# The opening of a two-layer diffusion kernel: half of the first modulation quarter ahead, key weights by quarters, two conditioning units between keys and values, query weights split later

## The chip, the cores and the metric

One core of one Trainium2 chip. The metric is the device time of one execution in microseconds (us); times in the trace count from the start of the profiled span. Engines are named as in the profile: PE (TensorE), PEld (its weight loads), DVE (VectorE), ACT (ScalarE), POOL (GpSimd), SP (SyncE, which issues the loads here).

## What is computed

Two layers over 512 latent tokens and 256 context tokens of width 1024. The change lies in the first layer's attention, cut here to what matters:

```python
mx = split(silu(c) @ ada_w[0] + ada_b[0], 6)        # shift, scale, gate, shift, scale, gate
mc = split(silu(c_ctx) @ ada_w[0] + ada_b[0], 6)
h_x = rms_norm(x, norm1_g[0]) * (1 + mx[1]) + mx[0]
h_c = rms_norm(ctx, norm1_g[0]) * (1 + mc[1]) + mc[0]
q, k, v = split(h_x @ w_qkv, [1024, 1280])          # 16 query heads, 4 key and value heads of 64
k_c, v_c = split(h_c @ w_qkv[:, 1024:], 2)          # context keys and values
q, k = rope(rms_norm(q, q_gain)), rope(rms_norm(k, k_gain))
out = softmax(window and context scores, sink) @ values @ w_o
```

After it come a SwiGLU feed-forward part, and a second layer with retention. The output is the latent stream.

## The kernel before, in words

Streams are held transposed, as 8 tiles of 128 channels by tokens (`res`). Products are done in three passes: a weight tile is split into a rounded part `whi` and a rest `wlo` (a cast on ACT, a subtraction on DVE), the moving operand likewise, and whi x hi, wlo x hi, whi x lo are summed in PSUM (`mm3`).

The opening goes through these steps. Eight latent tiles are loaded; ACT squares them, DVE adds the squares (`add_square`, L210, L211), and PE multiplies the sum with a matrix of ones (`rms`, L218); ACT and DVE make the normalising factor from it (`neg_half_rstd`, L101, L196 to L198). The modulation of the first norm (shift and scale) comes in four quarters of 256 channels: `ada_quarter` multiplies a quarter's four loaded tiles (`adan`) with the conditioning columns `ccol` (32 small matmuls, L338), ACT copies the result out (L341), PE turns it by two transposes (L345), and DVE adds the bias and makes the columns for one stream (L351, L352, L114). A function `fill` is issued between the product and the transposes. `hidden0` then makes two hidden tiles: DVE multiplies (L437), ACT adds the shift and rounds (L438), DVE makes the rest (L442). `keys(s, q)` (L451) adds what quarter q gives to the keys of stream s (0 latent, 1 context; 12 matmuls of 512 or 256 columns), `values(s, q, tiles)` (L465) the same for the values, 6 matmuls of 256 columns for each tile of 128 tokens. `high` and `low` (L380, L383) split the key and value weights; `busy` (L422) issues matmuls whose result nobody reads, to fill PE's waits. The order of all this on PE, DVE and ACT is the order in which the code is written (`tc.manual_schedule`).

Behind it a second block fixes PE alone: the last values, four conditioning units (`ada_unit`, L308 product, L311 copy, L315 transpose, L318 columns on DVE), the factors of the three key tiles (`key_factor`, L562) and the key operands (`key_parts`, L571 to L575). From there a scheduler orders the engines by dependencies and place in the program. `make_q` gives for a pair of heads the query tile as four pieces: `first`, `second` and `third` are the products for latent and context (L148 to L150) and `shape` (L628 and L629 on ACT read the product, L633 to L636 apply the rotary positions, L642 to L645 split the result), `norms` is six tiny matmuls (L654) that sum the squares, and DVE steps that end the use of their PSUM bank (L657). Pieces are placed among the steps of the attention blocks (`steps`); the query weights are loaded and split (L140 on ACT, L141 on DVE) when `make_q` is called. PSUM tiles named `pj` are two banks in turn: a third use waits for the readers of the first. The raw weight tiles `wraw` are two buffers in turn, and SP issues all loads in program order.

## Time and profile before

| what | value |
| --- | --- |
| median of 3 runs | 1747.66 us (1744.28 to 1747.7) |
| the profiled execution: its own time, its span | 1748.38 us, 1746.6 us |
| mean granted PE clock of the span | 0.997 |
| PE, DVE, ACT busy | 1717.8, 1335.8, 845.3 us |
| loads of the first 44 us: DMA share, first 19.71 us and then to 43.96 us | 0.90, 0.98 |

A row of the timeline gives the start in us, the busy time in us, engine, line, operation, the tiles out<-in with their shape, the number of instructions, and in brackets how long the engine had been idle and which engine, tile and line (or which load) released it. A PE matmul shows its whole latency as busy, so the start of the next one tells how fast they follow. A row of the stages gives the stretch, its length, the busy time and count of PE, PEld, DVE, ACT and POOL, the granted PE clock, the mean DMA share and GB/s.

### The profile page before, as it was taken

To read this page: it belongs to the slowest core of one execution; us is meant where nothing else is said; L and a number is where in the kernel's file an instruction comes from. 1 tells how busy PE (TensorE), PEld (TensorE's weight loads), DVE (VectorE), ACT (ScalarE), POOL (GpSimd) and SP (SyncE) were. 2 spreads that over 40 slices of the span, in tenths; PEclk is the share of its full clock that TensorE was granted. 3 is DMA by queue.
4 is the path that set the end of the run, shared out by engine and by line. 5 is a ranking of instruction groups with operands and counts; after the bars stand their busy time and mean duration, and the time that the engine had idled before them with its cause. 6 is when DMAs were issued, how large, how long until landed. Compare 5 with 4: busy or idle time off the path is not lost.

```text
span 1746.6 us, 28180 instructions
## 1 busy us (share of the span) xinstructions
PE 1717.8 (98%) x11092; PEld 1537.3 (88%) x11092; DVE 1335.8 (76%) x2382; ACT 845.3 (48%) x1509; POOL 121.2 (7%) x266
## 2 busy tenths in 40 slices
PE   7999999999999999999998999999999999999999
PEld 5888887889999999999998888898898999999997
DVE  5797786478778787877899758758768898777774
ACT  5577686365434333342565534624525555445442
POOL 0023344000000000000010000000000100000000
PEclk9999999999999999999999999999999999999999
DMA  9510024142243434343433434433433224233322
GB/s 365 206 61 16 23 61 146 49 141 101 97 133 122 144 121 157 109 145 110 140 115 122 157 97 134 157 109 123 157 103 115 97 87 124 80 116 102 105 77 85
DMA packets 61476, 205.67 MB, mean 118 GB/s; under 512 B 6816, under 2 KB 7456, under 8 KB 61216
## 3 DMA queue, kind: packets, MB, share of 16 engines
q1 hardware_dynamic: 54432, 178.71, 31.1%
q0 software_dynamic: 6912, 25.17, 4.7%
q8 instruction: 87, 1.43, 0.3%
q14 instruction: 45, 0.37, 0.1%
HBM read 201.75 MB, written 2.10 MB: 117 GB/s over the span
## 4 chain that ended last, share of the span: by engine, by line
PE 42%; DVE 6%; DMA 2%; ACT 1%; issue 0%; ACTq 0%; DVEq 0%; SPq 0%
PE Y L935 6%; PE Z L1338 6%; PE Z L935 3%; PE Y L1325 3%; PE pj L149 2%; PE pj L148 2%; PE pj L150 2%; PE pj L1338 2%; DMA wraw<-in_wst_dram 2%; PE X L935 2%; PE X L1325 1%; DVE wlo L1257 1%; PE X L1338 1%; PE X L150 1%; PE X L148 1%; PE X L149 1%
## 5 line engine op out<-in xcount | busy, mean ns | idle before, releaser
L165 ACT CAST whi<-wraw 128x1024 fp32r<-128x1024 f32 x117 | 122.4, 1052 | 208.4 <-PE Z L150 71.0
L935 PE MATMUL Y<-aq,whi 128*128 128x384 f32 x640 | 174.0, 336 | 2.1 <-ACT hn L1080 2.1
L166 DVE TENSOR_TENSOR wlo<-wraw,whi 128x1024 fp32r<-128x1024 f32 x117 | 142.5, 1222 | 16.1 <-ACT whi L165 15.7
L254 DVE SCALAR_TENSOR_TENSOR res<-pj,mod,res 128x512 f32<-128x512 f32 (+1 forms) x102 | 74.3, 729 | 78.5 <-PE pj L150 77.5
L935 PEld LDWEIGHTS Y<-aq,whi 128*128 128x128 f32 x640 | 116.7, 188 | 4.1 <-ACT hn L1080 3.9
L141 DVE TENSOR_TENSOR wlo<-wraw,whi 128x1024 fp32r<-128x1024 f32 x76 | 92.7, 1221 | 27.8 <-ACT whi L140 26.8
L140 ACT CAST whi<-wraw 128x1024 fp32r<-128x1024 f32 x76 | 79.7, 1048 | 70.0 <-PE Z L150 24.8
L935 PE MATMUL Y<-aq,wlo 128*128 128x384 f32 x320 | 107.0, 334 | 0.0
L272 DVE CUSTOM_DVE_ANT_0 y<-adaw,crow,small_sb 128x1024 bf16<-128x1024 f32 x64 | 81.9, 1279 | 31.3 <-DMA adaw<-in_adaT_dram 31.1
L1256 ACT CAST whi<-wraw 128x1024 fp32r<-128x1024 f32 x56 | 58.7, 1050 | 74.1 <-PE Y L150 52.6
L1257 DVE TENSOR_TENSOR wlo<-wraw,whi 128x1024 fp32r<-128x1024 f32 x56 | 68.0, 1220 | 18.0 <-ACT whi L1256 17.8
L1338 PE MATMUL Z<-whi,sA 128*128 128x512 f32 x256 | 80.4, 390 | 0.0
L101 ACT ACTIVATE pr<-pr,stat,qs 128x513 f32<-128x513 f32 (+2 forms) x96 | 74.1, 775 | 10.9 <-DVE stat L732 9.6
L739 POOL TENSOR_SCALAR pr<-pr,stat 128x512 f32<-128x512 f32 (+2 forms) x96 | 66.5, 705 | 73.1 <-DVE stat L736 48.9
L148 PE MATMUL pj<-ax,whi 128*128 128x512 f32 x176 | 68.8, 391 | 0.5 <-DVE res L254 0.5
L150 PE MATMUL pj<-ax,whi 128*128 128x512 f32 x176 | 68.7, 390 | 0.0
L149 PE MATMUL pj<-ax,wlo 128*128 128x512 f32 x176 | 68.5, 389 | 0.0
L269 POOL DMA_DIRECT2D adaw<-in_adaT_dram x48 | 25.6, 533 | 515.4 <-DVE mod L272 421.8
L935 PE MATMUL Y<-sA,whi 128*128 128x256 f32 x304 | 60.6, 282 | 0.0
L935 PEld LDWEIGHTS Y<-aq,wlo 128*128 128x128 f32 x320 | 60.1, 188 | 0.1
L148 PE MATMUL pj<-act,whi 128*128 128x512 f32 (+1 forms) x156 | 60.0, 384 | 0.0
L149 PE MATMUL pj<-act,wlo 128*128 128x512 f32 (+1 forms) x156 | 59.9, 384 | 0.0
(583 smaller groups left out, 5428.0 us busy)
## 6 DMA issues: line engine op xcount, KB each, us to landing
wraw<-in_wst_dram SPq DMA_DIRECT2D x232, 512.0 KB, 3.7
adaw<-in_adaT_dram POOLq DMA_DIRECT2D x48, 512.0 KB, 3.9
wx<-in_wst_dram SPq DMA_DIRECT2D x28, 512.0 KB, 4.4
adan<-in_adaQ_dram SPq DMA_DIRECT2D x16, 512.0 KB, 7.7
adan<-in_adaN_dram SPq DMA_DIRECT2D x16, 512.0 KB, 7.1
res<-in_xT_dram SPq DMA_DIRECT2D x16, 256.0 KB, 4.9
q<-in_adaN_dram SPq DMA_DIRECT2D x16, 256.0 KB, 3.6
aq<-in_adaN_dram SPq DMA_DIRECT2D x12, 256.0 KB, 5.7
```

Of the source, the lines that this page charges most:

```text
L140: after(nc.scalar.copy(hi, raw), behind)
L141: after(nc.vector.tensor_tensor(lo, raw, hi, op=sub), low)
L148: after(nc.tensor.matmul(o, whi, xhi, start=first, stop=False), behind)
L149: nc.tensor.matmul(o, wlo, xhi, start=False, stop=False)
L150: return nc.tensor.matmul(o, whi, xlo, start=False, stop=last)
L165: nc.scalar.copy(hi, t)
L166: return nc.vector.tensor_tensor(lo, t, hi, op=sub)
L254: return nc.vector.scalar_tensor_tensor(res[d], o, mods[l, s][:, part, d:d + 1], res[d], mult, add)
L272: after(nc.vector.tensor_tensor_reduce(junk, w, cr[:, s * 1024:(s + 1) * 1024], 1.0, sm_t[:, C_ADAB + l * 48 + j:C_ADAB + l * 48 + j + 1], ...
L935: ins = nc.tensor.matmul(o, p, r, start=first and k + i == 0, stop=k == 3 and i == 2, skip_group_check=not first)
L1257: last_split[0] = nc.vector.tensor_tensor(lo, raw, hi, op=sub)
L1338: ins = nc.tensor.matmul(o, p, r, start=first and k + i == 0, stop=k == 3 and i == 2, skip_group_check=not first)
```

## The change

The opening is written in another order, and some pieces are cut smaller:

- The first quarter is done in halves by `first_quarter`. Its scale half is loaded first, multiplied, copied out by DVE and turned, and only then its shift half is multiplied, copied out by ACT and turned.
- The last of the eight squares is no longer added by DVE: PE multiplies it with the ones by itself, and adds the product of the sum of the other eight in the same bank. One `busy(SX)` goes.
- Key weights 0 and 1 are loaded and split by 256, 256 and 512 columns (before 256 and 768), and their loads change places with the context tiles'.
- `values`, `hidden0`, `rms(1)` and the context keys are placed otherwise; conditioning units 0 and 1 move from behind the last latent values to between the last keys; context values of quarters 0 and 1 move the other way.
- The raw weights of query tile 0 are loaded into two key tiles and not into a `wraw` buffer. The weights of query tiles 2 and up are split when a fifth piece, `weights`, is called: at once for tile 2, at step 2 of the group for the second tile of a group, and three steps ahead of the group for its first.

In the opening, PE's list was this up to the first key products (`y_241` is the sum of squares, `sq` in L345 the copy of the quarter):

```order
L422 MATMUL kvv<-res,ones_sb 128x512 x4
L218 MATMUL pT<-y_241,ones_sb 128x512
L338 MATMUL pT<-adan,ccol 32x128 x32
L422 MATMUL kvv<-res,ones_sb 128x256
L345 MATMUL pT<-const_sb,sq 128x128 x2
L422 MATMUL kvv<-res,ones_sb 128x512 x2
L451 MATMUL pj<-h,whi 128x512 x2
```

In the changed kernel PE's list at the same place is this (`sc` are the copies of the two halves, L335 the products, L480 the keys):

```order
L449 MATMUL kvv<-res,ones_sb 128x512 x4
L521 MATMUL pT<-sq,ones_sb 128x512
L522 MATMUL pT<-y_245,ones_sb 128x512
L335 MATMUL pT<-adan,ccol 32x128 x16
L353 MATMUL pT<-const_sb,sc 128x128
L335 MATMUL pT<-adan,ccol 32x128 x16
L449 MATMUL kvv<-res,ones_sb 128x256
L353 MATMUL pT<-const_sb,sc 128x128
L449 MATMUL kvv<-res,ones_sb 128x512
L480 MATMUL pj<-h,whi 128x512 x2
```

The transpose of the scales now stands between the two halves of the product. DVE's list at this place was before, from the last additions to the first hidden tiles (`hs`):

```order
L211 TENSOR_TENSOR y_241<-y_241,sq 128x512 x7
L197 SCALAR_TENSOR_TENSOR sq<-pT,sq 128x512
L198 SCALAR_TENSOR_TENSOR y_241<-sq,y_241 128x512
L351 TENSOR_TENSOR mod_74<-pT,small_sb 128x2x2
L352 TENSOR_TENSOR mod_74<-pT,mod_74 128x2x2
L114 SCALAR_TENSOR_TENSOR acol_78<-mod_74,gm_85 128x2
L437 SCALAR_TENSOR_TENSOR hs<-res,acol_78,y_241 128x512 x2
```

DVE's list there in the changed kernel:

```order
L211 TENSOR_TENSOR y_245<-y_245,sq 128x512 x6
L197 SCALAR_TENSOR_TENSOR sq<-pT,sq 128x512
L198 SCALAR_TENSOR_TENSOR y_245<-sq,y_245 128x512
L357 COPY sc<-pT 128x128
L343 TENSOR_TENSOR mod_74<-pT,small_sb 128x2
L344 TENSOR_TENSOR mod_74<-pT,mod_74 128x2
L114 SCALAR_TENSOR_TENSOR acol_78<-mod_74,gm_85 128x2
L464 SCALAR_TENSOR_TENSOR hs<-res,acol_78,y_245 128x512
L343 TENSOR_TENSOR mod_74<-pT,small_sb 128x2
L344 TENSOR_TENSOR mod_74<-pT,mod_74 128x2
L464 SCALAR_TENSOR_TENSOR hs<-res,acol_78,y_245 128x512
```

The copy of the scales stands behind both steps of the norm's factor, and the shift's two steps stand between the first and the second hidden tile. The second place is the second query tile (heads 2 and 3), behind the first one's sums of squares (`qs`). DVE had before, up to the end of those sums' use (L657):

```order
L197 SCALAR_TENSOR_TENSOR qs<-pj,qs 128x12
L575 TENSOR_TENSOR k<-res,k 64x512
L644 TENSOR_TENSOR q<-hn,q 64x512
L645 TENSOR_TENSOR q<-hn,q 64x512
L644 TENSOR_TENSOR q<-hn,q 64x256
L645 TENSOR_TENSOR q<-hn,q 64x256
L198 SCALAR_TENSOR_TENSOR qs<-qs 128x12
L574 TENSOR_TENSOR k<-res,k 64x512
L657 SCALAR_TENSOR_TENSOR qs<-pj,qs 128x12
```

DVE has now, up to the same step (L699) and on to the second tile's rotary step (L678) and a score (L773):

```order
L197 SCALAR_TENSOR_TENSOR qs<-pj,qs 128x12
L619 TENSOR_TENSOR k<-res,k 64x512
L198 SCALAR_TENSOR_TENSOR qs<-qs 128x12
L141 TENSOR_TENSOR wlo<-wraw,whi 128x1024
L699 SCALAR_TENSOR_TENSOR qs<-pj,qs 128x12
L675 STREAM_SHUFFLE y_1238<-hn 128x512
L703 TENSOR_SCALAR qs<-qs,nsink 128x6 x2
L676 TENSOR_TENSOR hn<-hn,rope_192 128x512
L677 TENSOR_TENSOR y_1238<-y_1238,rope_192 128x512
L773 ISA pr,stat<-S_1353,mask,qs 128x512
L773 ISA stat 128x1
L678 TENSOR_TENSOR hn<-hn,y_1238 128x512
```

A whole weight split (L141) stands ahead of L699 now, and a score ahead of the rotary sum L678. ACT had before, for the second query tile's product (`hn`, `sq`) and what followed:

```order
L628 ACTIVATE hn<-pj,qk_gain 128x512
L629 ACTIVATE sq<-pj 128x512
L628 ACTIVATE hn<-pj,qk_gain 128x256
L629 ACTIVATE sq<-pj 128x256
L101 ACTIVATE qs<-pj,small_sb 128x12
L101 ACTIVATE qs<-qs 128x12
L196 ACTIVATE qs<-qs 128x12
L642 CAST q<-hn 64x512
```

ACT has now:

```order
L670 ACTIVATE hn<-pj,qk_gain 128x512
L671 ACTIVATE sq<-pj 128x512
L670 ACTIVATE hn<-pj,qk_gain 128x256
L684 CAST q<-hn 64x512
L685 CAST q<-hn 64x512
L671 ACTIVATE sq<-pj 128x256
L684 CAST q<-hn 64x256
L685 CAST q<-hn 64x256
L101 ACTIVATE qs<-pj,small_sb 128x12
```

The context square L671 stands behind two casts that read L678's result. The diff, cut to its core:

```diff
     def ada_quarter_load(q):
-        w = []
-        for i in range(4):
-            w.append(T(st_p, 1024, "adan", 8))
+        w = [T(st_p, 1024, "adan", 8) for _ in range(4)]
+        for i in (2, 3, 0, 1) if q == 0 else range(4):
             nc.sync.dma_start(w[i], adaQ[q, i // 2, i % 2])
         return w
 
+    def quarter_product(o, w, part, ks):
+
+        for k2 in ks:
+            for j in range(4):
+                k = 2 * k2 + j // 2
+                c0 = (k % 4) * 256 + j % 2 * P
+                nc.tensor.matmul(o[32 * j:32 * j + 32, part * P:(part + 1) * P], ccol[:, k, :],
+                                 w[2 * part + k // 4][:, c0:c0 + P], start=k2 == 0, stop=k2 == 3)
+
+    def quarter_columns(q, t, s, parts=(0, 1)):
+        tv = t.rearrange("p (f h d c) -> p c h f d", f=2, h=2, d=2)
+        bias = sm_t[:, C_ADAB:C_ADAB + 16].rearrange("p (f d) -> p f d", f=2)[:, :, 2 * q:2 * q + 2]
+        f = slice(parts[0], parts[-1] + 1)
+        col = mods[0, s][:, f, 2 * q:2 * q + 2]
+        nc.vector.tensor_tensor(col, tv[:, s, 0, f], bias[:, f], op=add)
+        nc.vector.tensor_tensor(col, tv[:, s, 1, f], col, op=add)
+        if 1 in parts:
+            fold_gain(0, s, 0, 2 * q, 2 * q + 2)
+
+    def first_quarter(w, fill):
+
+        o, t = pT()[:, 0:256], pT()[:, 0:256]
+
+        def turn(part, rows):
+            nc.tensor.transpose(t[:, part * P:(part + 1) * P], rows, ident)
+
+        quarter_product(o, w, 1, range(4))
+        scales, shifts = (T(st_p, SC, "sc", 2)[:, :P] for _ in range(2))
+        nc.vector.tensor_copy(scales, o[:, P:])
+        turn(1, scales)
+        quarter_columns(0, t, 0, (1,))
+        quarter_product(o, w, 0, range(4))
+        nc.scalar.copy(shifts, o[:, 0:P])
+        fill()
+        turn(0, shifts)
+        return lambda: quarter_columns(0, t, 0, (0,)), lambda: quarter_columns(0, t, 1)
+
     def ada_quarter(q, w, fill):
 
         o = pT()[:, 0:256]
         for part in range(2):
-            for k2 in range(4):
-                for j in range(4):
-                    k = 2 * k2 + j // 2
-                    c0 = (k % 4) * 256 + j % 2 * P
-                    nc.tensor.matmul(o[32 * j:32 * j + 32, part * P:(part + 1) * P], ccol[:, k, :],
-                                     w[2 * part + k // 4][:, c0:c0 + P], start=k2 == 0, stop=k2 == 3)
+            quarter_product(o, w, part, range(4))
         rows = t_sq(256)
         nc.scalar.copy(rows, o)
         fill()
         t = pT()[:, 0:256]
         for part in range(2):
             nc.tensor.transpose(t[:, part * P:(part + 1) * P], rows[:, part * P:(part + 1) * P], ident)
...
     res0[1] = load_stream(1, 0, 4)
     wq.append(ada_quarter_load(1))
+    load_cols(0, quarters[1])
+    load_cols(1, quarters[1])
     res0[1] += load_stream(1, 4)
-    load_cols(0, REST)
-    load_cols(1, REST)
     load_cols(2, BACK)
+    load_cols(0, BACK)
+    load_cols(1, BACK)
     wq.append(ada_quarter_load(2))
...
-    q_raw = [w_raw()]
+    q_raw = [key_room()]
+    for i, c in enumerate((HEAD, BACK)):
+        nc.sync.dma_start(q_raw[0][i], wst[wpos[0]][:, c])
+    wpos[0] += 1
     wu = [unit_load(u) for u in UNITS[:2]]
...
             nc.vector.scalar_tensor_tensor(ts[-1], res0[s][k], acol[0, s, 0][:, k:k + 1], y, mult, mult)
+            for b in early if k == ks[0] else ():
+                b()
             nc.scalar.activation(h[s][k][0], ts[-1], AF.Identity, bias=mods[0, s][:, 0, k:k + 1])
...
     with tc.manual_schedule(engines={mybir.EngineType.PE, mybir.EngineType.DVE, mybir.EngineType.Activation}):
-        squares0(0, *range(KT))
+        squares0(0, *range(KT - 1))
+        last_square = t_sq(SX)
+        nc.scalar.activation(last_square, res0[0][KT - 1], AF.Square)
         for k in range(4):
             busy(SX, k)
-        rms(0, bank=pT)
+        tot = pT()
+        nc.tensor.matmul(tot, ones, last_square, start=True, stop=False)
+        nc.tensor.matmul(tot, ones, ssq[0], start=False, stop=True)
+        neg_half_rstd(ssq[0], t_sq(SX), tot, D)
 
         def first_fill():
             high(0, quarters[0])
             high(1, quarters[0])
             busy(SC)
 
-        c1 = ada_quarter(0, wq[0], first_fill)
+        c0, c1 = first_quarter(wq[0], first_fill)
         busy(SX)
-        busy(SX)
-        hidden0(0, 0, 1, between=(lambda: low(0, quarters[0]), lambda: low(1, quarters[0])))
+        hidden0(0, 0, 1, between=(lambda: low(0, quarters[0]), lambda: low(1, quarters[0])), early=(c0,))
         high(2, HEAD)
         c1()
         keys(0, 0)
         low(2, HEAD)
         squares0(1, 0, 1, 2, 3)
-        c1 = ada_quarter(1, wq[1], lambda: values(0, 0, (0,)))
-        high(0, REST)
-        values(0, 0, (1, 2, 3))
-        hidden0(0, 2, 3, between=(lambda: low(0, quarters[1]), lambda: high(1, REST), lambda: low(1, quarters[1])))
+        values(0, 0, (0,))
+        c1 = ada_quarter(1, wq[1], lambda: values(0, 0, (1,)))
+        high(0, quarters[1])
+        high(1, quarters[1])
+        values(0, 0, (2, 3))
+        hidden0(0, 2, 3, between=(lambda: low(0, quarters[1]), lambda: low(1, quarters[1])))
         c1()
         high(2, BACK)
         low(2, BACK)
         squares0(1, 4, 5, 6, 7)
+        high(0, BACK)
+        high(1, BACK)
+        low(0, quarters[2])
+        low(1, quarters[2])
         keys(0, 1)
         values(0, 1, (0, 1))
+        c1 = ada_quarter(2, wq[2], lambda: values(0, 1, (2,)))
+        hidden0(0, 4, 5)
         rms(1, bank=pT)
-        c1 = ada_quarter(2, wq[2], lambda: values(0, 1, (2,)))
         values(0, 1, (3,))
-        hidden0(0, 4, 5, between=(lambda: low(0, quarters[2]), lambda: low(1, quarters[2])))
-        c1()
         high(3, HEAD)
         low(3, HEAD)
+        c1()
+        keys(0, 2)
         hidden0(1, 0, 1)
-        keys(0, 2)
-        keys(1, 0)
-        values(0, 2, (0, 1, 2))
-        hidden0(1, 2, 3)
         low(0, quarters[3])
         low(1, quarters[3])
-        c1 = ada_quarter(3, wq[3], lambda: values(0, 2, (3,)))
+        c1 = ada_quarter(3, wq[3], lambda: values(0, 2, (0,)))
         c1()
         hidden0(0, 6, 7)
+        values(0, 2, (1, 2, 3))
+        keys(1, 0)
+        hidden0(1, 2, 3)
         high(3, BACK)
+        end = ada_unit(UNITS[0], wu[0])
+        keys(0, 3)
+        end()
+        hidden0(1, 4, 5)
+        keys(1, 1)
+        end = ada_unit(UNITS[1], wu[1])
+        hidden0(1, 6, 7)
         low(3, BACK)
-        keys(1, 1)
-        values(1, 0)
-        values(1, 1)
-        hidden0(1, 4, 5)
-        hidden0(1, 6, 7)
-        keys(0, 3)
         keys(1, 2)
+        end()
         last_key = keys(1, 3)
...
         after(values(0, 3), [last_key])
-        ends = [ada_unit(UNITS[0], wu[0])]
+        ends = [ada_unit(UNITS[2], wu[2])]
         rope_key(kn[0])
-        values(1, 2)
-        ends.pop()()
-        ends.append(ada_unit(UNITS[1], wu[1]))
         key_factor(0)
+        values(1, 0)
         ends.pop()()
         for e in range(2):
             kx[e] = key_parts(e, kn[0])
+        values(1, 1)
+        ends.append(ada_unit(UNITS[3], wu[3]))
+        key_factor(1, pO)
+        values(1, 2)
+        ends.pop()()
+        off_grid(akv, 16)
+        for e in range(2):
+            k1, k2 = key_parts(e, kn[1], "kc", 4)
+            kc[e], kc[2 + e] = ((k1[:, c], k2[:, c]) for c in HALVES)
+        off_grid(akv, 48)
         values(1, 3)
+        rope_key(kn[2])
+        key_last = key_factor(2)
         vt = []
         for t in range(6):
             v = T(akv, 256, "v", 6)
             nc.scalar.copy(v, kvv[t // 2][:, t % 2 * 256:t % 2 * 256 + 256])
             vt.append(v)
-        ends.append(ada_unit(UNITS[2], wu[2]))
-        key_factor(1)
-        off_grid(akv, 16)
-        for e in range(2):
-            k1, k2 = key_parts(e, kn[1], "kc", 4)
-            kc[e], kc[2 + e] = ((k1[:, c], k2[:, c]) for c in HALVES)
-        off_grid(akv, 48)
-        ends.pop()()
-        ends.append(ada_unit(UNITS[3], wu[3]))
-        rope_key(kn[2])
-        key_last = key_factor(2, pO)
-        ends.pop()()
...
+        def weights():
+            w.extend(cut(next_w(ap, 1, raw, behind, behind)))
+
         def first():
+            if not w:
+                weights()
             part(0, 0, 5)
...
-            steps[12 * g + r] = list(fs)
+            steps.setdefault(12 * g + r, []).extend(fs)
+        if g == 0:
+            a[4]()
+        else:
+            steps.setdefault(12 * g - 3, []).append(a[4])
+        steps.setdefault(12 * g + 2, []).append(b[4])
```

32 lines of the change are left out of this document (14 added, 18 removed).

## The prediction

> **What bounds the kernel now.** I read the page first (busy shares and slices), then a table of the stages of the opening, then the timelines of PE, DVE and ACT where PE waits. On the page:
>
> ```profile
> PE 1717.8 (98%) x11092; PEld 1537.3 (88%) x11092; DVE 1335.8 (76%) x2382; ACT 845.3 (48%) x1509; POOL 121.2 (7%) x266
> PE   7999999999999999999998999999999999999999
> ```
>
> PE is busy for 98% of the span, and only the first slice of 43.7 us falls below nine tenths. The profiled execution took 1748.38 us, of which the span is 1746.6. The lists of all engines agree from inside the attention stage on, before 330 us, so the change can act only ahead of that. The table of stages:
>
> ```profile
> 0.00:19.71 19.71, 12.53 (x82) 5.53 (x82) 9.03 (x21) 12.59 (x20) 0.64 (x9) 1.00 0.90 327
> 19.71:43.96 24.25, 21.63 (x218) 16.37 (x218) 16.93 (x45) 11.46 (x24) 0.00 (x0) 1.00 0.98 391
> 43.96:64.06 20.10, 19.62 (x198) 18.47 (x199) 14.63 (x41) 10.91 (x24) 0.00 (x0) 1.00 0.64 226
> 64.06:87.81 23.75, 23.46 (x340) 18.12 (x339) 18.05 (x47) 15.14 (x30) 0.00 (x0) 1.00 0.49 187
> 87.81:101.37 13.56, 12.25 (x82) 11.01 (x81) 13.20 (x27) 9.58 (x19) 0.30 (x2) 1.00 0.17 49
> 101.37:330.00 228.63, 227.04 (x1681) 182.98 (x1681) 171.12 (x557) 155.81 (x372) 83.29 (x190) 0.99 0.17 56
> ```
>
> The stages are the first norm and quarter; three quarters of latent keys and values; the rest of the keys; units and key operands with query tile 0; query tile 1; attention. Behind 43.96 PE idles little, except for 1.3 us in 87.81:101.37, where DVE is busy 13.20 of 13.56 us: there DVE sets the pace. What the change can win lies ahead of 44 us; whether it is kept is decided at 87 to 101 us.
>
> PE's rate isn't the busy time of one matmul, as two neighbours show:
>
> ```profile
> 84.07 0.39 PE L150 MATMUL pj<-h,k 128*128 128x512 f32 x1
> 84.30 0.39 PE L148 MATMUL pj<-h,k 128*128 128x512 f32 x1
> ```
>
> They start 0.23 us apart (0.235 over a long row of them), so 12 key products of 512 columns are 2.82 us; a value tile, 6 products of half the columns, I take at 0.71.
>
> **Step 1, the opening chain: +0.85 us.** PE, then DVE, then ACT:
>
> ```profile
> 12.45 1.13 PE L218 MATMUL pT<-y,ones_sb 128*128 128x512 f32 x2 [1.69 <-DVE y L211]
> 13.51 1.84 PE L338 MATMUL pT<-adan,ccol 128*32 128x128 f32 x48
> 15.95 0.64 PE L338 MATMUL pT<-adan,ccol 128*32 128x128 f32 x16 [0.60 <-DMA adan<-in_adaQ_dram]
> 17.09 0.44 PE L345 MATMUL pT<-const_sb,sq 128*128 128x128 f32 x2
> 19.71 0.50 PE L451 MATMUL pj<-h,whi 128*128 128x512 f32 x1 [0.47 <-ACT h L438]
> ```
>
> ```profile
> 16.38 0.69 DVE L198 SCALAR_TENSOR_TENSOR y<-sq,y 128x512 f32<-128x512 f32 x1
> 17.56 0.16 DVE L351 TENSOR_TENSOR mod<-pT,small_sb 128x4 f32<-128x4 f32 x1 [0.49 <-PE pT L345]
> 18.15 1.41 DVE L437 SCALAR_TENSOR_TENSOR hs<-res,acol,y 128x512 f32<-128x512 f32 x2
> ```
>
> ```profile
> 10.84 0.63 ACT L210 ACTIVATE sq<-res 128x512 f32<-128x512 f32 x1 [0.17 <-DVE y L211]
> 18.94 1.38 ACT L438 ACTIVATE h<-hs,mod 128x512 fp32r<-128x512 f32 x2 [1.29 <-DVE hs L437]
> 66.08 0.27 ACT L311 COPY sq<-pT 128x128 f32<-128x128 f32 x1 [1.27 <-PE pT L308]
> ```
>
> The last square is done at 11.47. Before, a last addition on DVE and one product with the ones follow, up to about 13.6. After, two such products (about 1 us each) follow from 11.5, also to about 13.6: the saved addition buys the added product, gain 0. The norm's two DVE steps end at 17.07 as before. The copy of the scales stands behind them on DVE. No row shows a 128x128 copy on DVE: it lies between 0.16 (the 128x4 step) and 0.69 (512 columns); I take 0.29, next to ACT's 0.27 for the same shape. It ends at 17.4, and here PE's order costs: the scale transpose (0.27) comes after that, and only then the shift half of the product, which before was over at 16.6. The 64 products took 1.84 + 0.64 less overlap, 1.9 in all; half is 0.94. So the shift product ends at 18.66, ACT copies to 18.99, PE turns to about 19.35 behind `busy`, DVE adds twice to 19.75 and makes the second `hs` by 20.47; ACT's first hidden tile ends about 20.5 and the first key product starts at 20.56 instead of 19.71. Bounds: +0.4 if the copy is 0.16 and PE's queue flows, +1.2 at 0.69. The ACT casts of key weights there are hidden under the wait for the shift; without it they would be 0.7.
>
> **Step 2, 19.71 to 43.96: -2.25 us.** Rows of PE:
>
> ```profile
> 23.09 1.96 PE L338 MATMUL pT<-adan,ccol 128*32 128x128 f32 x64
> 25.79 0.38 PE L345 MATMUL pT<-const_sb,sq 128*128 128x128 f32 x2
> 28.36 0.50 PE L451 MATMUL pj<-h,whi 128*128 128x512 f32 x1
> 34.63 0.67 PE L218 MATMUL pT<-y,ones_sb 128*128 128x256 f32 x2 [0.45 <-DVE y L211]
> 40.50 0.49 PE L451 MATMUL pj<-h,whi 128*128 128x512 f32 x1 [1.48 <-ACT h L438]
> 44.42 0.79 PE L451 MATMUL pO<-hc,whi 128*128 128x256 f32 x2 [0.46 <-ACT hc L438]
> ```
>
> The stage's work is three key quarters (8.46), eight value tiles (5.68), two quarter products (3.8), two pairs of transposes (0.5) and the context norm (0.6): 19.0 us of 24.25, so 5.2 are waits (more than the idle rows say, since an isolated matmul shows as 0.5 busy). Between transposes and first key product of a quarter lie 28.36 - 26.17 = 2.2 us (copying, columns, two hidden tiles on DVE and ACT). After, two value tiles (1.42) stand in quarter 1's gap, and the norm and one tile (1.3) in quarter 2's, leaving 0.75 and 0.85. About 0.45 each stays in the three key quarters, where a second hidden tile follows a first; more was there while the 768-column casts stood between. Left: 0.45 + 0.75 + 0.46 + 0.85 + 0.46, about 3.0; 5.25 - 3.0 = 2.25. Gone are the 1.48 at 40.50 and the norm's 0.45. Bounds: 1.2, if what DVE does between (the 1.2 us splits in the same queue) stretches the two gaps by 0.5 each, and 3.2, if only half a microsecond stays in each gap.
>
> **Step 3, 43.96 to 87.81: -1.85 us.** The work is the same in another order, 41.8 us by the rates. Of 43.85 us 2.0 are waits and tails; the 0.46 at 44.42 goes, since values stand ahead of the context keys, and the load's wait in the next row goes with the other tails, as units stand between keys:
>
> ```profile
> 73.94 0.65 PE L308 MATMUL pT<-adan,ccol 128*32 128x128 f32 x16 [0.29 <-DMA adan<-in_adaN_dram]
> 89.69 0.61 PE L654 MATMUL pj<-const_sb,sq 128*128 128x2 f32 x4 [0.84 <-ACT sq L629]
> 90.16 0.48 PE L148 MATMUL pj<-h,whi 128*128 128x512 f32 x1
> ```
>
> This asks unit 0's weights some 24 us earlier. Ahead of them and in them are about 16 MB; at 327 and then 391 GB/s the stages' rows give 15.9 MB by 43.96, so they land about 47, needed at 49; unit 1 (another 2 MB, 5 us) about 52.5, needed at 55. The margins are 2 to 3 us, and this is what the swapped key and context loads live on too: if they miss, PE waits by as much. I take 0 for that, bound +1. By steps 1 to 3 the first query tile's sums of squares end near 86.7, against 90.16 before: 3.45 ahead: 3.25 by the three steps, and 0.2 off the 0.84 that PE waits for the last square, which ACT reaches with one cast less ahead of it.
>
> **Step 4, query tile 1, 87 to 101: +2.25 us given back.** DVE:
>
> ```profile
> 88.18 0.73 DVE L633 STREAM_SHUFFLE y<-hn 128x512 f32<-128x512 f32 x1
> 88.80 1.21 DVE L141 TENSOR_TENSOR wlo<-wraw,whi 128x1024 fp32r<-128x1024 f32 x1
> 92.66 0.67 DVE L575 TENSOR_TENSOR k<-res,k 64x512 fp32r<-64x512 f32 x1
> 96.62 0.17 DVE L657 SCALAR_TENSOR_TENSOR qs<-pj,qs 128x12 f32<-128x12 f32 x1
> ```
>
> PE and ACT at its end:
>
> ```profile
> 96.94 0.36 PE L148 MATMUL pj<-hc,whi 128*128 128x256 f32 x1 [0.47 <-DVE qs L657]
> 101.37 0.47 PE L148 MATMUL pj<-h,whi 128*128 128x512 f32 x1
> ```
>
> ```profile
> 100.33 0.38 ACT L629 ACTIVATE sq<-pj 128x256 f32<-128x256 f32 x1
> ```
>
> From the first tile's shuffle to the end of L657 DVE needs 8.61 us; PE's context half waits for that end (0.47), as the bank is in use. Now one more weight split (1.21) and one key part (0.70) fall between: 10.5. The shuffle comes at about 83.5 (the key operands' work ends 4.7 earlier), so L699 ends at 94.15; PE stands there from 86.7 + 5.64 (24 products of 512 columns) + 0.95 (its other work) = 93.3: it waits 0.85. The context half ends near 97.0. Then ACT: the context square stands behind two casts that want L678, ahead of which DVE has shuffle 0.73, two small steps 0.36, two products 1.36, a score about 0.8 and the sum 0.69: 98.1. Two casts at the 0.63 of ACT's 512 columns and the square's 0.38 give 99.8, the last sums 0.45: 100.15 for the start of the third tile, against 101.37. Of 3.45 us 1.2 are left. Bounds: 0 given back, if PE reads other work in these waits, and 3.4, if L699 is a whole split later.
>
> **Step 5, the rest: 0.** Query tiles from the third on split their weights later; PE's stage of 228.63 us has only 1.6 idle, and the split is placed three steps of a group ahead, more than 10 us: hidden under the scores of other heads; one split late would cost 1.2. The loads there go past a queue used 0.17 of the time. Extra casts on ACT stand in its idle half.
>
> **Sum:** +0.85 - 2.25 - 1.85 - 0.2 at those sums (-3.45 at 86.7) + 2.25 = -1.2. Own time 1748.38 - 1.2 = 1747.2; the profiled execution stands 0.7 above the median 1747.66, so the median becomes **1746.5**.
>
> **Rivals.** *The clock drops (slower).* Rows of windows, with PE's busy time first behind the length and the granted clock third from the end:
>
> ```profile
> 9.92:13.33 3.41, 1.72 (x4) 0.30 (x2) 2.17 (x4) 1.26 (x2) 0.00 (x0) 1.00 1.03 417
> 951.99:955.40 3.41, 0.77 (x4) 0.31 (x2) 3.41 (x5) 0.32 (x2) 0.00 (x0) 1.00 0.46 142
> 955.40:958.82 3.42, 3.04 (x7) 2.47 (x8) 2.98 (x6) 2.09 (x4) 0.00 (x0) 0.50 0.77 246
> ```
>
> A window with PE half busy kept the clock; one with 23% is followed by a window at 0.50. The new order leaves PE idle from the end of the scale products, about 14.45, to 17.45: 3.0 us; in the window ahead of 955.40 it was idle for 2.6 of 3.41. If a window falls so that it is under some half busy, the following 3.4 us run at half, which doubles the transpose, the shift product and the next transpose: +1.5; a second such window at tile 1's last sums, where PE now waits about 2.5 us, adds at most 1.7. That gives -1.2 + 3.2 = +2.0, **1749.7** (1748.0 with the first alone); it ends above before as soon as the clock's price passes 1.2. Against it: `busy` products ahead of 13.6 and the 50% row. The Trainium skill, "TensorE: Matmul & The Clock Gate", section "Why this matters for your kernels", says to avoid gaps of PE over about 3 us between bursts of matmuls, and so speaks against this change; by it the sum would be that of this rival, without it the forecast's; the 0.50 row behind 955.40 agrees.
>
> *All is given back.* DVE has no slack in 87.81:101.37 (13.20 of 13.56). If L699 stands one key part later and the score's scan is longer, by 1.2 together, the third tile starts where it did: **1747.7**.
>
> *More is kept.* If the scheduled DVE work lies in waits it had anyway, step 4 gives nothing back: -3.4, **1744.3**. For it speaks that DVE gets its key operands earlier; against it the list, which has one split more ahead of L699.
>
> **How the numbers follow.** The forecast has 0.36 (1745.6 to 1747.2), the clock 0.20, all given back 0.22, more kept 0.18; 0.02 go to each side beyond. The range 1743.2 to 1749.8 leaves out the lower part of the last case and the tails, with the bounds of steps 1 to 3 (each about 1) inside. 0.2% is 3.5 us, about what a measurement of this kernel can tell from no change: below 1744.2 lies 0.15 (most of the case of more kept), above 1751.2 0.05 (the clock with a late load), between them 0.80.
>
> **What would show it.** Right: the first key product at 20.5 with the shift product behind the scale transpose at 17.5; quarter 2's first keys without the 1.48 wait; the first query sums about 3.4 us earlier; then PE waiting for `qs` L699 and for `sq` L671, and the third tile about 1.2 earlier. Wrong: a first key product before 20 or after 21, PE waiting for `adan` of units 0 or 1, a granted clock of 0.50 in 15 to 25 or 95 to 102, or no waits at L699 and L671.

## The result and the profile after

The changed kernel took 1749.97 us (median of 12 runs, 1746.58 to 1752.42) against 1746.14 before (12 runs, 1744.06 to 1747.7): a ratio of 1.0021, 95% interval 1.0014 to 1.0029, so slower by 2.4 to 5.1 us. Beside later experiments it was run once more: 1750.37 against 1748.11, ratio 1.0010 (1.0001 to 1.0019). The forecast was 1746.5 with a range up to 1749.8: the sign was wrong, and the time lies just outside. As a difference the miss is larger, 3.8 us slower instead of 1.2 faster: the forecast counted from 1747.66, the median of three executions, and the twelve beside the changed kernel have 1746.14. The profiled execution took 1751.12 us with a span of 1749.3. The page's first line of the changed kernel:

```profile
PE 1715.7 (98%) x11092; PEld 1538.4 (88%) x11092; DVE 1334.7 (76%) x2384; ACT 844.3 (48%) x1511; POOL 121.9 (7%) x266
```

PE is busy 2.1 us less in a span that is 2.7 us longer: PE waits more. The opening on PE, from the timeline of the changed kernel (start, busy time, then engine, line and tiles; some rows left out):

```profile
13.33 1.08 PE L335 MATMUL pT<-adan,ccol 128*32 128x128 f32 x32
17.16 0.47 PE L353 MATMUL pT<-const_sb,sc 128*128 128x128 f32 x1 [2.74 <-DVE sc L357]
17.56 1.94 PE L335 MATMUL pT<-adan,ccol 128*32 128x128 f32 x32
19.43 1.22 PE L449 MATMUL kvv<-res,ones_sb 128*128 128x256 f32 x2
20.44 0.42 PE L353 MATMUL pT<-const_sb,sc 128*128 128x128 f32 x1
22.06 1.41 PE L480 MATMUL pj<-h,whi 128*128 128x512 f32 x2
```

The order is the forecast's: scale product, a wait of 2.74 us for DVE's copy of the scales, the transpose, the shift product. But the two halves of the product are equal work, and the first took 1.08 us, the second 1.94. The windows of the changed kernel say why (length, busy time of PE, PEld, DVE, ACT and POOL, granted clock, DMA):

```profile
13.03:16.44 3.41, 1.39 (x33) 0.81 (x32) 0.92 (x2) 1.95 (x3) 0.00 (x0) 1.00 1.04 404
16.45:19.86 3.41, 2.71 (x34) 2.01 (x35) 1.88 (x6) 0.30 (x2) 0.00 (x0) 0.50 1.05 422
19.87:23.27 3.40, 3.40 (x7) 1.62 (x7) 2.34 (x7) 2.55 (x6) 0.00 (x0) 0.50 1.03 408
```

PE was busy for 41% of the window up to 16.44, and the next two ran at half clock. The first key product starts at 22.06, where the forecast had 20.56 and before had 19.71.

The stages after, first key product to the end of three latent key quarters, to the second query tile, to the third:

```profile
22.06:45.27 23.21, 21.08 (x220) 17.13 (x219) 16.18 (x41) 11.30 (x25) 0.00 (x0) 0.97 1.04 412
45.27:89.35 44.08, 43.04 (x550) 38.47 (x549) 36.78 (x97) 29.36 (x58) 0.00 (x0) 1.00 0.48 179
89.35:102.83 13.48, 10.97 (x70) 9.75 (x70) 13.13 (x27) 8.05 (x18) 1.25 (x2) 1.00 0.27 80
```

Against before they take 1.0 us less (24.25), 2.1 less (from 43.96 to 90.16 it was 46.20) and 2.3 more (from 90.16 to 101.37 it was 11.21). So the third query tile starts 1.46 us later than before instead of 1.2 earlier. PE's two waits at the second query tile, on its timeline, and the third tile's first product:

```profile
97.19 0.35 PE L148 MATMUL pj<-hc,whi 128*128 128x256 f32 x1 [1.18 <-DVE qs L699]
102.37 0.61 PE L696 MATMUL pj<-const_sb,sq 128*128 128x2 f32 x4 [1.33 <-ACT sq L671]
102.83 0.48 PE L148 MATMUL pj<-h,whi 128*128 128x512 f32 x1
```

Both are waits that the forecast had. In attention PE's waits were these before, longest ones first:

```profile
PE pO L773 <- DVE tt L751: 0.3, 1, 0.3
PE pj L654 <- ACT sq L629: 0.3, 1, 0.3
PE pT L745 <- POOL pr L739: 0.3, 1, 0.3
```

and these after (total, times, longest one; both views are from 101 to 300 us):

```profile
PE pT L792 <- POOL pr L786: 2.0, 4, 0.8
PE pj L696 <- ACT sq L671: 1.3, 1, 1.3
PE pT L906 <- DMA q<-in_adaN_dram: 0.9, 1, 0.9
```

The wait for `sq` is the one just shown; the 2.0 us for POOL in the attention blocks the forecast had not.

### The profile page after: what moved, and what is told of

The parts are those of the page before. It is cut to its first block, busy times and chain, and to the rows that moved or that the text cites. A ratio compares the mean times of both kernels' runs of the same rounds, so it can differ in the third digit from the quotient of the medians.

```text
span 1749.3 us, 28191 instructions
## 1 busy us (share of the span) xinstructions
PE 1715.7 (98%) x11092; PEld 1538.4 (88%) x11092; DVE 1334.7 (76%) x2384; ACT 844.3 (48%) x1511; POOL 121.9 (7%) x266
## 4 chain that ended last, share of the span: by engine, by line
PE 40%; DVE 7%; DMA 2%; ACT 1%; issue 1%; ACTq 0%; DVEq 0%; SPq 0%
PE Z L1390 6%; PE Y L987 6%; PE Y L1377 3%; PE Z L987 3%; PE pj L150 2%; PE pj L149 2%; PE pj L148 2%; PE pj L1390 2%; DMA wraw<-in_wst_dram 2%; PE X L987 2%; PE X L1377 1%; DVE wlo L1309 1%; PE X L1390 1%; PE X L149 1%; PE X L150 1%; PE X L148 1%
## 5 line engine op out<-in xcount | busy, mean ns | idle before, releaser
L166 DVE TENSOR_TENSOR wlo<-wraw,whi 128x1024 fp32r<-128x1024 f32 x117 | 142.6, 1222 | 16.1 <-ACT whi L165 15.8
L141 DVE TENSOR_TENSOR wlo<-wraw,whi 128x1024 fp32r<-128x1024 f32 x76 | 92.8, 1223 | 27.3 <-ACT whi L140 26.4
```

Source lines behind the costliest of these rows:

```text
L141: after(nc.vector.tensor_tensor(lo, raw, hi, op=sub), low)
L166: return nc.vector.tensor_tensor(lo, t, hi, op=sub)
```

## How the experiments are read

Runs of one kernel spread over some 6 us, and an interval of the ratio is about 0.0018 wide (3 us): medians tell only the larger differences apart. The ratio is estimated from all executions and isn't the quotient of the two medians (that would be 1.0011 for e10 and 1.0013 for the changed kernel run again). The trace is finer up to the end of attention: two profiles of the changed kernel have the first key product at 22.06 and 22.02, the third query tile at 102.83 and 102.78, and one DVE step behind the last waits (`hc`, L166, called the mark here) at 286.43 and 286.49. The mark of before, then of the changed kernel:

```profile
284.97 0.29 DVE L166 TENSOR_TENSOR hc<-pO,hc 128x128 fp32r<-128x128 f32 x1 [1.78 <-ACT hc L165]
```

```profile
286.43 0.29 DVE L166 TENSOR_TENSOR hc<-pO,hc 128x128 fp32r<-128x128 f32 x1 [1.78 <-ACT hc L165]
```

Behind the mark the code is the same, and the same order can differ by 0.9 us ahead of it too (e8 and e10 below). From the mark to the end of the span the two profiles of the changed kernel differ by 1.4 us, and all profiles lie between 1458.0 (e7) and 1464.3 (changed, again); half-clock windows come there as well, two in the changed kernel and none of full length in e7. Whether a part of the change's price falls behind the mark isn't settled: the medians differ by more than the marks do. All runs, with the half-clock windows that lay ahead of the mark:

| kernel | median | before beside it | ratio (95%) | first key | 3rd query tile | mark | half clock from |
| --- | --- | --- | --- | --- | --- | --- | --- |
| before | 1746.14 | | | 19.71 | 101.37 | 284.97 | 115.7 |
| changed | 1749.97 | 1746.14 | 1.0021 (1.0014-1.0029) | 22.06 | 102.83 | 286.43 | 16.4, two |
| changed, again | 1750.37 | 1748.11 | 1.0010 (1.0001-1.0019) | 22.02 | 102.78 | 286.49 | 16.4, two |
| e1 PE kept busy | 1749.48 | 1747.12 | 1.0018 (1.0009-1.0028) | 20.48 | 100.84 | 284.51 | none |
| e2 copy first | 1748.11 | 1747.12 | 1.0006 (0.9997-1.0015) | 19.29 | 100.04 | 285.18 | 87.6, 101.3 |
| e3 early weights | 1745.35 | 1747.12 | 0.9995 (0.9987-1.0004) | 20.97 | 100.31 | 282.91 | 18.6 |
| e4 before, late weights | 1749.31 | 1747.12 | 1.0015 (1.0006-1.0023) | 19.51 | 101.41 | 287.15 | 41.2, 116.3 |
| e5 e3 with copy first | 1744.15 | 1746.38 | 0.9986 (0.9978-0.9995) | 18.92 | 98.18 | 281.09 | 87.1 |
| e6 e3 with old opening | 1744.32 | 1746.38 | 0.9987 (0.9978-0.9996) | 20.51 | 99.76 | 282.65 | 12.9, 88.0 |
| e7 e3 with PE busy | 1745.06 | 1746.38 | 0.9991 (0.9982-1.0000) | 20.50 | 99.81 | 282.68 | 87.5 |
| e8 tile 3 early | 1748.29 | 1746.38 | 1.0009 (1.0000-1.0019) | 20.58 | 100.22 | 284.57 | 18.8 |
| e9 tiles 2-5 early | 1747.33 | 1748.11 | 0.9996 (0.9987-1.0006) | 20.46 | 99.85 | 285.11 | 87.9 |
| e10 late ones sooner | 1749.98 | 1748.11 | 1.0003 (0.9994-1.0012) | 20.47 | 99.82 | 285.05 | 87.4 |

## The experiments

**e1, the gap filled.** Theory: the clock fell because PE stood still behind the scale product. Rival: whatever is won there is given back at the second query tile.

```diff
         nc.vector.tensor_copy(scales, o[:, P:])
+        for k in range(3):
+            busy(SX, k)
         turn(1, scales)
```

> The changed kernel with three products whose result nobody reads between the scale product and the scale transpose, where PE idled from 14.41 to 17.16. Clock theory: the granted clock stays at 1.00 from 16.45 to 23.28 (it was 0.50 there), the shift product takes 0.95 us and not 1.94, the first key product starts at 20.4 to 20.7 and not at 22.06, the first query tile's sums are some 1.8 us earlier, and as DVE's chain behind them moves with PE's, the time falls by 1.5 to 2 us against the changed kernel (some 1748.2). Rival, all given back: DVE sets the pace at the second query tile, so the first key product is earlier but the third query tile's first product still stands at 102.5 to 102.8, and the time is within 0.4 us of the changed kernel's.

PE's timeline of e1:

```profile
14.38 2.84 PE L451 MATMUL kvv<-res,ones_sb 128*128 128x512 f32 x6
17.20 0.33 PE L353 MATMUL pT<-const_sb,sc 128*128 128x128 f32 x1
17.46 1.08 PE L335 MATMUL pT<-adan,ccol 128*32 128x128 f32 x32
20.48 0.50 PE L482 MATMUL pj<-h,whi 128*128 128x512 f32 x1 [0.34 <-ACT h L469]
```

The transpose comes no earlier (17.20), but the shift product takes 1.08 and the first key product starts at 20.48, 1.58 us earlier. The third query tile starts 1.99 earlier, the mark lies 1.92 earlier: nothing is given back, the rival falls. The median doesn't show it (ratio 1.0018 against the changed kernel's 1.0021 and 1.0010). So the windows' price is read from the trace, some 1.9 us in an execution that has two of them. The granted clock of all executions says why the median moves less: its mean is 0.9967 for the changed kernel (23 executions) and 0.9973 for e1 (10). One half-clock window lowers the mean by 0.0010 (half of 3.41 us in 1750), so on average the filled gap saves about half a window, not two. One profile without a window is no proof either, as two of the six profiles with the gap have none ahead of the keys; but of the four with the gap filled or shortened (e1, e2, e5, e7) none has one.

**e2, the copy first.** Theory: the copy stands behind the norm's two steps on DVE, and that alone makes the gap.

```diff
         turn(1, scales)
         quarter_columns(0, t, 0, (1,))
+        factor()
         quarter_product(o, w, 0, range(4))
...
-        tot = pT()
+        tot = kvv[0]
...
-        neg_half_rstd(ssq[0], t_sq(SX), tot, D)
...
-        c0, c1 = first_quarter(wq[0], first_fill)
+        c0, c1 = first_quarter(wq[0], first_fill, lambda: neg_half_rstd(ssq[0], t_sq(SX), tot, D))
```

> The changed kernel with the copy of the scales, and the scale's columns, ahead of the norm's two DVE steps (the sum's product goes to a bank of its own, so that the transpose has one free). Theory that the copy's place cost the opening: the scale transpose moves from 17.16 to about 14.8, the shift product ends by 16.6 with the loads, PE idles less than a window in one piece, the clock stays at 1.00, and the first key product starts at 18.5 to 19.0 instead of 22.06; the first query sums are about 3 us earlier. Of these, theory 'moves with it' keeps 2.5 to 3 us to the end (some 1747), theory 'all given back' at most 0.5. If the shift's loads land later than 16, the first key product comes at 19.5 or later.

PE's timeline of e2:

```profile
15.19 0.33 PE L353 MATMUL pT<-const_sb,sc 128*128 128x128 f32 x1 [0.41 <-DVE sc L357]
15.45 1.20 PE L335 MATMUL pT<-adan,ccol 128*32 128x128 f32 x32
19.29 0.50 PE L481 MATMUL pj<-h,whi 128*128 128x512 f32 x1 [1.04 <-ACT h L468]
```

The wait shrinks from 2.74 to 0.41 us, and the first key product is 2.8 us earlier (19.29, behind the 18.5 to 19.0 expected; the sums started 0.4 us later in this execution). The third query tile keeps 2.8 us of it. The mark keeps 1.25, but a half-clock window lay at 101.3 here; with the early weights (e5 below, no such window there) it keeps 1.8 of 2.1.

**e3, the query weights early.** Theory: the weights split late cause the new waits for POOL. This undoes that part alone: loads and splits when a tile is made.

```diff
-        w = w or []
+        w = w or cut(next_w(ap, 1, raw, behind, behind))
...
-            steps.setdefault(12 * g + r, []).extend(fs)
-        if g == 0:
-            a[4]()
-        else:
-            steps.setdefault(12 * g - 3, []).append(a[4])
-        steps.setdefault(12 * g + 2, []).append(b[4])
+            steps[12 * g + r] = list(fs)
```

> The changed kernel with the query weights of tiles 2 and up loaded and split as before, when the tile is made, and not in a piece of their own. Theory that the late splits cost PE its waits in attention (the waits for POOL at 154.6, 244.8 and 263.8 and for a load at 277.8, 2.7 us together, where before had 0.26): those waits go, and the time falls by 2 to 2.7 us against the changed kernel; the second query tile behaves as before the change or a little worse (one more split in DVE's list ahead of its rotary step). Rival, they are the shift of everything by other lengths: the waits stay at about 2 us in other places, and the time is within 0.5 us of the changed kernel's.

PE's waits from 101 to 300 us in e3:

```profile
PE pT L787 <- POOL pr L781: 0.5, 2, 0.3
PE S L767 <- DVE stat L768: 0.4, 1, 0.4
PE pT L901 <- DMA q<-in_adaN_dram: 0.3, 1, 0.3
```

2.0 us for POOL are down to 0.5, and the time falls from 1.0021 (1.0010 in the repetition) to 0.9995. The mark is 3.52 us earlier than the changed kernel's, of which 1.1 came with one half-clock window less at the opening (first key product at 20.97). The rest has two places. From third query tile to mark e3 takes 182.60 us, the changed kernel 183.60: 1.0. And at the second query tile it takes 12.1 and not 13.5: 1.4, which was in neither theory. ACT's timeline there, of the changed kernel first, then of e3:

```profile
100.29 0.47 ACT L670 ACTIVATE hn<-pj,qk_gain 128x256 f32<-128x256 f32 x1 [4.01 <-PE pj L150]
100.66 0.60 ACT L684 CAST q<-hn 64x512 fp32r<-64x512 f32 x1
101.29 0.61 ACT L685 CAST q<-hn 64x512 fp32r<-64x512 f32 x1
101.93 0.38 ACT L671 ACTIVATE sq<-pj 128x256 f32<-128x256 f32 x1
```

```profile
99.04 0.47 ACT L670 ACTIVATE hn<-pj,qk_gain 128x256 f32<-128x256 f32 x1 [3.90 <-PE pj L150]
99.42 0.38 ACT L671 ACTIVATE sq<-pj 128x256 f32<-128x256 f32 x1
99.68 1.05 ACT L140 CAST whi<-wraw 128x1024 fp32r<-128x1024 f32 x1
100.61 0.62 ACT L684 CAST q<-hn 64x512 fp32r<-64x512 f32 x1
```

With the weights of tile 3 split early the square for the last sums stands ahead of the two casts, and PE's 1.33 us for it are gone.

**e4, the late weights alone, in the kernel before.** The reverse of e3's edit, in the kernel before.

> The kernel before with only the late query weights: loads and splits of tiles 2 and up in a piece of their own. Theory that the late splits cost: slower than before by 1.5 to 2.7 us, with waits of PE for POOL's pr between 145 and 280. Rival: within 0.5 us of before, and then the loss of the whole change comes from the opening and the second query tile alone. The first key product stands at 19.7 in either.

Ratio 1.0015 (1.0006 to 1.0023), and the mark 2.18 us later, though the third query tile stands where it did (101.41, 101.37). Both profiles have a half-clock window at 116, so it isn't that. PE's waits:

```profile
PE pT L750 <- POOL pr L744: 1.9, 3, 0.8
PE S L730 <- DVE stat L731: 0.6, 1, 0.6
PE pj L654 <- ACT sq L629: 0.4, 1, 0.4
```

The same 1.9 us for POOL, without anything else of the change. How the longest of them comes about is seen around the split of tile 6's weights. DVE of the changed kernel, then POOL's multiplications of `pr` and PE's wait:

```profile
153.70 0.16 DVE L783 RECIPROCAL stat<-stat 128x2 f32<-128x2 f32 x1
153.77 1.20 DVE L141 TENSOR_TENSOR wlo<-wraw,whi 128x1024 fp32r<-128x1024 f32 x1
```

```profile
151.33 0.48 POOL L786 TENSOR_SCALAR pr<-pr,stat 128x256 f32<-128x256 f32 x1 [2.06 <-DVE stat L779]
153.96 1.37 POOL L786 TENSOR_SCALAR pr<-pr,stat 128x256 f32<-128x256 f32 x1 [1.69 <-DVE stat L783]
155.38 1.00 PE L792 MATMUL pT<-const_sb,pr 128*128 128x128 f32 x4 [0.81 <-POOL pr L786]
```

POOL's operation at 153.96 has its reciprocal (153.70) ahead of the split, so it doesn't stand behind it in any queue. But it runs while DVE does the split, and takes 1.37 us where the same operation took 0.48 at 151.33; it ends at 155.32, and PE's transposes start at 155.38. The other long wait is like it (DVE, POOL, PE):

```profile
262.24 1.24 DVE L141 TENSOR_TENSOR wlo<-wraw,whi 128x1024 fp32r<-128x1024 f32 x1
261.77 1.97 POOL L786 TENSOR_SCALAR pr<-pr,stat 128x256 f32<-128x256 f32 x2 [1.24 <-DVE stat L783]
263.80 0.33 PE L792 MATMUL pT<-const_sb,pr 128*128 128x128 f32 x1 [0.73 <-POOL pr L786]
```

This is the tenth split in DVE's row, behind those of query tiles 1 to 7, so by its place one of the output projection's weights (`w_o`). In all eight profiles with late weights these two operations of POOL take 1.37 and 1.52 us. In e3 the sixth tile's split stands earlier and meets no work of POOL, whose next multiplication takes its 0.48:

```profile
146.11 1.22 DVE L141 TENSOR_TENSOR wlo<-wraw,whi 128x1024 fp32r<-128x1024 f32 x1
149.34 0.48 POOL L781 TENSOR_SCALAR pr<-pr,stat 128x256 f32<-128x256 f32 x1 [1.32 <-DVE stat L778]
```

So the wait goes with the split and POOL's operation at the same time; why POOL is slow then, no run here tests. An overlap costs only where PE wants the result at once: in e3 one at 266.36 takes 1.63 us beside a split, and PE has no such wait there. The third wait, 0.33 at 244.80, isn't the change's: before has one of 0.3 as well.

**e5, e6, e7: the opening, with the weights early.** e5 joins e2's and e3's edits; e6 joins e3's edit and the opening of before; e7 joins e1's and e3's edits.

> The changed kernel with both: query weights loaded and split as before, and the scales' copy and columns ahead of the norm's two DVE steps. If the two savings add up: first key product at about 19.3, first query sums some 1.7 us ahead of the run with the early weights alone, third query tile at 98 to 98.7, and 1 to 2 us below that run (some 1744, ratio to before 0.998 to 0.999). If what the opening saves is given back at the second query tile (DVE sets the pace there): the third tile at 99.5 or later, and the same time as that run.

> The changed kernel with the query weights as before and also the opening as before (whole first quarter, seven additions, a single product with the ones), so that of the change the key weights by quarters, the units between keys and the raw weights in key tiles are left. By the prediction's step 1 (+0.85 for the halves) the first key product stands at 19.5 to 19.9, no window of half clock ahead of it, and the time is 0.8 to 2 us below the run with the early weights alone (ratio to before 0.998 to 0.999). If the halves are no loss: first key product the same or the time equal or above.

> The changed kernel with the query weights as before and three products that nobody reads in the gap ahead of the scale transpose. Clock theory: no half-clock window in the first 25 us, first key product at 20.5, and the median about 0.5 to 1.5 us below the run with the early weights alone, since that one shows such a window in some of its runs. Rival: as windows of half clock come elsewhere too (at the sums of query tiles), the median stays within 0.4 us of it.

e5: first key product at 18.92, third query tile at 98.18, ratio 0.9986 (0.9978 to 0.9995): the savings add up, and this is, with e6, the lowest ratio of all, below both kernels. e6: 0.9987; its first key product stood at 20.51, since a half-clock window lay ahead of it in this profile, where before and e4, with the same opening, had 19.71 and 19.51. The halves as the change has them are no gain in the trace: without a half-clock window ahead of it the first key product stands at 20.46 and 20.47 with them (e9, e10) and at 19.71 and 19.51 without, as step 1 said. By the ratios the time without them is 1.4 us lower than e3's (0.9987 against 0.9995), though the intervals overlap. e7: 20.50, 0.9991, between.

**e8, e9, e10: which late split.** e8 splits tile 3 at once too; e9 the tiles 2 to 5; e10 is e8 with the later pieces three steps sooner.

```diff
         if g == 0:
             a[4]()
+            b[4]()
         else:
-            steps.setdefault(12 * g - 3, []).append(a[4])
-        steps.setdefault(12 * g + 2, []).append(b[4])
+            steps.setdefault(12 * g - 6, []).append(a[4])
+            steps.setdefault(12 * g - 1, []).append(b[4])
```

(e10; e8 has 3 and 2 as before, e9 the condition `g < 2`.)

> The changed kernel with the weights of the first group's second tile (tile 3) loaded and split at once, as before, and only those of later groups late. If each late split makes its own wait: PE's wait of 0.80 for POOL at 154 goes, those of 0.33 and 0.73 (245 and 264) stay, ACT has the context square ahead of the casts at the second query tile again or not as the scheduler orders it, and the time falls by 0.8 to 2.5 us against the changed kernel. If the waits come from the later groups: the time stays within 0.5 us and the wait at 154 stays.

> The changed kernel with the weights of query tiles 2 to 5 (the first two groups) loaded and split at once, as before, and only those of tiles 6 and 7 late. If the wait of 0.80 at 154 comes from the late split of tile 4 (which stood on DVE at 153.8): it goes, the waits at 245 and 264 stay, and the time is 0.5 to 1.5 us below the run with tile 3 alone early (ratio to before 1.0000 to 1.0005). If all three waits come from the last group: they stay, and the time equals that run's (1.0009).

> The changed kernel with tile 3 early and the later splits in pieces of their own but three steps (some 14 us) sooner. If their place so near to the scores of the same step makes the waits for POOL: with another place the 0.80, 0.33 and 0.73 go or come elsewhere with less than 1 us in all, and the time is near that of the run with all weights early (ratio 0.9995 to 1.0000). If any late split costs, wherever it is put (the scheduler ranks it behind the scores): the waits stay at 1.5 us or more and the ratio at 1.0006 to 1.0012.

In e8 the second query tile takes 12.2 us again, so its 1.3 go with tile 3's late split; but the wait at 154, which I had put down to the same split, stays. In e9 it still stays, with tiles 2 to 5 early. e9's waits:

```profile
PE pT L792 <- POOL pr L786: 1.8, 3, 0.8
PE pT L906 <- DMA q<-in_adaN_dram: 1.1, 2, 0.7
```

So the split at 153.8 is the sixth tile's and not the fourth's, as its place in the row of splits says too, and the wait at 264 comes with a split of the output projection. What the second query tile wins is lost again in attention: from third query tile to mark e8, e9 and e10 take 184.35, 185.26 and 185.23 us, the changed kernel 183.60 and e1 183.67; and e10's mark (285.05) is not ahead of e1's (284.51), neither with a half-clock window ahead of the keys. Where that goes isn't found.

e10 doesn't test what it was made for. All engines have e8's order in it, instruction for instruction: three steps sooner in the program moved no split (tile 6's stands at 152.14, in e9 at 152.15). The scheduler puts it there, 51 us ahead of the tile's first product (153.77 and 204.88 in the changed kernel), whatever the piece's step. So whether another place would do stays open. As a second run of e8's program e10 shows how far the figures go: ratios of 1.0009 and 1.0003, and marks of 284.57 and 285.05, with a wait for a load of 0.43 at 267.46 in e8 and of 1.01 at 276.37 in e10. e9's ratio (0.9996) below both is within these limits.

**e11, the changed kernel again**, without an edit.

> The changed kernel once more, unaltered, for a second profile beside the other runs of this call. The waits for POOL at 154 to 264 and the third query tile's 2.3 us for 13.5 against 11.2 come again to within 0.2 us if they are set by the order; the half-clock windows at the opening come at another place or not at all if their grid is free against the program, and the first key product then stands at 20.4 to 20.6 (no window) or 20.9 to 22.1. The ratio to before is 1.0014 to 1.0029 as before.

Waits, second query tile and both half-clock windows came again to within 0.1 us. The windows do move in other kernels: with this same order of the opening they came twice here, once in e3 and e8 (from 18.6 and 18.8), and not at all in e9 and e10, whose first key product stood at 20.46 and 20.47. With the gap filled or shortened (e1, e2, e5, e7) none came ahead of the keys.

## Why the prediction was wrong, point by point

Reckoned at the mark, the changed kernel is 1.46 us behind before. Before had a half-clock window at 115.7; from third query tile to mark it took 183.60 us, where e3, which has its weights early as well and no window there, took 182.60 (e5 to e7 182.87 to 182.91). Taking 1.0 as that window's price, an estimate, the change costs 2.5, and the forecast was -1.2: 3.7 to explain. (A window at 101.3 made the same stretch of e2 1.5 longer than e1's, whose order is the same there: 185.14 against 183.67. By that it would be 4.2.) The medians differ by 3.8 (2.4 to 5.1); what lies between them and the mark isn't located.

- **Step 5, cost 0: the step that failed.** "One split late would cost 1.2", hidden by a lead of more than 10 us: I looked at when a split is needed, and not at what runs beside it. No split was late (those of tiles 3 to 7 stood 18 to 51 us ahead of their first use). POOL's operations that ran beside one took 1.37 and 1.52 us instead of 0.48, and PE waited 0.81 and 0.73 for them. In attention the late splits cost 1.0 us by e3 (183.60 against 182.60) and 0.8 by e1 and e7, which differ by e3's edit alone (183.67 against 182.87); in e4 it is 2.1. With what they add at the second query tile e7's mark is 1.8 ahead of e1's. By the times their undoing is the largest single effect (1.0021 and 1.0010 to 0.9995, and 1.0018 to 0.9991 from e1 to e7), and alone they make the kernel before slower (1.0015). ACT's "idle half" was misread besides: the row has it busy for 155.81 of 228.63 us.
- **Step 1, +0.85: right, but for the clock.** The copy of the scales took 0.28, the transpose stood at 17.16 (17.45 forecast), and without the drop of the clock the first key product stands at 20.46 to 20.48 (e9, e10, e1; 20.56 forecast). The drop was the first rival's, at the place it named, and for a window under some half busy: 41% here. It was put at +1.5 by the first window; two came, and the whole cost is 1.9 at the second query tile (89.35 against e1's 87.46), in this execution the largest of the terms. I gave it 0.20; of six profiles with this opening four had it. That the rival's 1749.7 stands next to the measured 1749.97 is luck: its second window, +1.7 at the tile's last sums, didn't come, the late splits aren't in it, and it counts from 1747.66.
- **Step 2, -2.25: too large by 0.9.** In the execution without the drop (e1) the stage takes 22.89 us (20.48 to 43.37), 1.36 less than before. The two gaps are near what was worked out (0.75 and 0.85), as PE's timeline of the changed kernel shows ahead of the second and third quarter's keys:

```profile
31.70 0.49 PE L480 MATMUL pj<-h,whi 128*128 128x512 f32 x1 [0.76 <-ACT h L467]
41.88 0.50 PE L480 MATMUL pj<-h,whi 128*128 128x512 f32 x1 [1.04 <-ACT h L467]
```

  But a value tile between other products takes 0.8 us (from 25.63 to the next quarter's product at 26.43), not 0.71, and there are eight. Before the change it was so too (from 37.12 to the transposes at 37.93), so less of its 24.25 us was waiting than the step took for granted.
- **Step 3, -1.85 with 0.2: right.** From 45.27 to 89.35 PE took 44.08 us, 2.1 less than before. No load of a unit was waited for: the cover held.
- **Step 4, +2.25 given back: right in size (2.27), and in its waits** (1.18 for `qs` L699, 0.85 expected; 1.33 for `sq` L671), but not in its whole cause: 1.3 of it goes when tile 3 is split early (e8), and 1.0 is left. It isn't a give-back of a lead either: it came with a lead of 0.8 as it would have with 3.45, and of what e1, e2 and e5 won at the opening nearly all went through it (of e2's 3.1 at the second tile 2.8 were left at the third). The rival "all is given back" falls with that.

Sum: 1.0 (step 5) + 1.9 (clock) + 0.9 (step 2) - 0.1 (steps 1 and 3) = 3.7, and 0 from step 4.

## What to carry to other kernels

A piece of work that is moved to a place "in good time" still runs beside other work there: ask what it meets at its new place, on its own engine and on the others, not only when its result is wanted. And look in the trace for where it came to stand: three steps sooner in the program moved nothing here. Where an operation is put into the order by hand, look at what its engine has ahead of it that isn't ready: the copy behind two steps that waited for a square cost more than the halving could win, and the same halves with the copy ahead were, with the old opening, the fastest version. A lead was nearly kept through a stage that another engine paces, as that engine's own start moved with it.

## What was not expected of the hardware

A gap of PE of 2.74 us, within a window of 41% busy, was enough for the clock to fall; 1.44 us busy of 3.41 ahead of e3's window and 1.33 ahead of e6's (with a gap of 2.08) were too, 1.72 of 3.41 in before was not. The Trainium skill, "TensorE: Matmul & The Clock Gate", section "Why this matters for your kernels", speaks of gaps over about 3 us; here less sufficed. The busy time of the profile alone doesn't decide it: in e9 the window up to 87.86 has PE busy for 2.37 of 3.41 us, and half clock follows; some 1.5 of it are the sums of squares, products of two columns each. And a second half-clock window followed in the changed kernel although PE was busy for 2.71 of 3.41 us in the first; at half clock that is 1.36 us of full-speed work, about as little as in the window before. That it is counted so is argued from these rows, not shown.

An operation of POOL can take three times as long while DVE does a weight split: 1.37 and 1.52 us against 0.48, in every profile with late weights.
